# A router rebuilt between two weight streams: logits finished in place, top two by counting, and a gather that comes out transposed

## The chip, the cores and the metric

The kernel runs on one core of a Trainium2 chip. The time is the device time of one execution, in microseconds. It has a TensorE (PE, matrix products; PEld its weight loads), a VectorE (DVE), a ScalarE (ACT), a GpSimd (POOL) and a SyncE (SP), whose queue issues nearly all transfers.

## What is computed

One decoder layer for 256 tokens of width 2048 in fp32. The first part (attention heads beside a gated recurrence) adds its result to x through `w_out`. Then comes a mixture of experts with two-stage routing, and the change lies between the two:

```python
h2 = rms_norm(x, norm_ffn_g)
grp_prob = softmax(h2 @ w_grp + b_grp)            # 4 groups
grp_w, grp_idx = lax.top_k(grp_prob, 1)           # one group
exp_logits = (h2 @ w_er + b_er)[that group]       # 4 experts in it
top_w, top_idx = lax.top_k(softmax(exp_logits), 2)
top_w = top_w / sum(top_w) * grp_w
for each of the 16 experts:
    hid = silu(h2 @ w_gate[e]) * (h2 @ w_up[e]) * combine[:, e]
    out = out + hid @ w_down[e]
x = rms_norm(x + out, final_norm_g)
```

Ties go to the lower index, as in `top_k`.

## The kernel before

**The first part's end.** The projection through `w_out` (`proj_n`, L366) works with split fp32 products: each raw 1 MB tile of weights is cut into a high and a low part (`units`, L319 and L321), and three products are made of them. It goes twice over the columns, once for each half of the contraction. In the second pass the blocks are 512, 512, 512, 256 and 256 columns wide, numbered 0 to 4. Work on a finished block (`out_block`, L688) is a generator in a queue `bgq`: it adds the block to X (L691), squares it for the norm (L694), transposes 128 columns at a time (L705), copies them (L708) and multiplies them with the router's weights (L711), two column groups of the logits at once, into the PSUM tile `pl`. `step(k)` advances the queue by k yields after each unit (L380), `drain()` empties it behind the last projection. All instructions go through a scheduler that keeps program order as priority on each engine, but may bring a ready instruction forward; `keep_in_program_order` forbids this for those so marked.

**The router.** `pl` is copied to SBUF (L735), folded and turned to tokens by two products (L738), scaled by the inverse norm `r2` and biased into `Z` (L746): for each token tile of 128 four groups of four expert logits and one of four group logits, 40 numbers a partition. `first_max` (L752 to L756) takes the first maximum of every four; it runs on `Z`, then, the winner pushed far down (L769), once more. `selb` (L774) holds the two chosen experts of the chosen group. Five small bf16 products count how many earlier tokens chose each expert (L776 to L780): the rank `rk` (L783) is the slot of a token with its expert; each expert has 64 slots (CAP), and a branch at the end, taken if one has more, is not taken with these inputs. `keep_busy` issues filling products on TensorE whose results nobody reads, at three places in this chain.

**The experts.** `gather_matrix(e)` (L846) makes a 0/1 matrix times the inverse norm from ranks. `gather` multiplies it with X, token rows on the output partitions (two column blocks side by side), and copies to SBUF (L860). `turn` transposes that (L834) and multiplies by the norm's gain (L873): `xg`, the expert's inputs with the contraction on the partitions. `stream` multiplies `xg` with four 2 MB pieces of `w_gate`, then of `w_up`. Then come silu (L957), the hidden product (L961), its transposes and copy (L967), and four pieces of `w_down` (`pd`). The result is scattered to tokens behind the next expert's first gate piece (L901). The gather for expert e+1 stands between up and down of expert e. `final_gain` spreads the final norm's gain over the partitions with 16 products, in expert 1 behind the third gate piece.

**The order of transfers.** The list `loads` is an order by hand. Twelve entries are loaded early, most beside the first part, as buffers come free. Piece 8 takes the two raw buffers of the first part as one tile. Later pieces go round a `ring` of nine 2 MB buffers: piece n from 12 on takes the buffer of the piece nine ring places before. Each is issued by `advance()` behind the products that read a piece, and waits in SP's queue for its buffer. Expert 0's last up piece lies outside the ring in a buffer that becomes `rest`, expert 0's hidden values among them.

Of the kernel before, what the change touches and what calls it, by code (L numbers as in the profile page):

```python
# [19 lines left out]
P = 128  # L20
# [17 lines left out]
def hybrid_block_kernel(  # L38
# [149 lines left out]
    rev = cst.tile([P, 4], F32, name="rev")  # L188
    nc.gpsimd.iota(rev, pattern=[[-1, 4]], base=4, channel_multiplier=0,
                   allow_small_or_imprecise_dtypes=True)  # L190
# [51 lines left out]
    def drain():  # L242
        while bgq:
# [6 lines left out]
                   (8, 8), (9, 9), (10, 7), (0, 1, 1)]  # L250
    ring = [d[1] for d in early_loads if len(d) == 2 and d[0] != 7]
# [17 lines left out]
    def load():  # L269
# [96 lines left out]
    def proj_n(aTh, aTl, c0=0, c1=NC, w=512):  # L366
# [3 lines left out]
        while c < c1:  # L370
            for hi, lo in units():
# [8 lines left out]
                step(2 if c0 else 1)  # L380
# [306 lines left out]

    def out_block(b, col, w, pp, last):  # L688
# [10 lines left out]
        for j in range(0, k, 2):  # L699
            xT = xTs[xi[0] % 2]  # L700
            xi[0] += 1
            pt = psmall().rearrange("p (j t) -> p j t", j=2)
            for i in range(2):
                for n in range(NT):
                    nc.tensor.transpose(  # L705
                        pt[:, i, n * P:(n + 1) * P],
                        x2[:, n, bs].rearrange("p (q j) -> p j q", j=k)[:, j + i], ident)
            V.tensor_copy(xT, pt)  # L708
            yield
            for i in range(2):  # L710
                mm(pl[32 * i:32 * i + 32], wr[:, col // P + j + i], xT[:, i],  # L711
                   start=b == 0 and j == 0, stop=b == 4)
# [16 lines left out]
    def keep_busy(k, ps, lhs, rhs):  # L729
        for i in range(k):  # L730
            mm(ps[0:lhs.shape[1], 0:P], lhs, rhs, start=True, stop=True)

    keep_busy(8, busy, ident, x2[:, 1, D - P:])
    lt = dist1[0:64]
    V.tensor_copy(lt, pl)  # L735
    plt = psmall()[:, :40].rearrange("p (n e) -> p n e", n=NT)
    for n in range(NT):
        mm(plt[:, n], lt[:, n * P:(n + 1) * P], fold[0:64], start=True, stop=True)  # L738


    r2 = small8[:, 2:4]
    V.tensor_reduce(r2, ssq, AX.X, ALU.add)
    rstd(r2, r2, D)
    Z = cst.tile([P, 5, NT, 4], F32, name="Z")
    for n in range(NT):
        V.scalar_tensor_tensor(Z[:, :, n], plt[:, n].rearrange("p (g e) -> p g e", g=5),  # L746
# [3 lines left out]
    def first_max(dst, src, m, tmp, vm, k):  # L750

        V.tensor_reduce(m, src, AX.X, ALU.max)  # L752
        V.tensor_tensor(tmp, src, m.unsqueeze(2).to_broadcast([P, k, 4]), ALU.is_equal)
        V.tensor_tensor(tmp, tmp, rev.unsqueeze(1).to_broadcast([P, k, 4]), ALU.mult)
        V.tensor_reduce(vm, tmp, AX.X, ALU.max)
        V.tensor_tensor(dst, tmp, vm.unsqueeze(2).to_broadcast([P, k, 4]), ALU.is_equal)  # L756

    Zf = Z.rearrange("p g n e -> p (g n) e")
    ma = cst.tile([P, 10], F32, name="ma")
    mb = cst.tile([P, 8], F32, name="mb")  # L760
    vm = cst.tile([P, 10], F32, name="vm")
    tmp = cst.tile([P, 10, 4], F32, name="tmp")
    M1 = cst.tile([P, 10, 4], F32, name="M1")
    M2 = cst.tile([P, 8, 4], F32, name="M2")
    E2 = cst.tile([P, 8, 4], F32, name="E2")
    keep_busy(8, busy, Z.rearrange("p g n e -> p (g n e)"), ident)
# [5 lines left out]
    gm = M1[:, 8:10].rearrange("p n g -> p g n").unsqueeze(3).to_broadcast([P, 4, NT, 4])  # L772
# [3 lines left out]
    mm(pr[:, 0], before, selb[:, :, 0], start=True, stop=True)  # L776
    mm(pr[:, 1], ones, selb[:, :, 0], start=True, stop=False)
    mm(pr[:, 1], before, selb[:, :, 1], start=False, stop=True)
    mm(pr[:, 2], ones, selb[:, :, 0], start=True, stop=False)
    mm(pr[:, 2], ones, selb[:, :, 1], start=False, stop=True)  # L780
# [6 lines left out]
    V.tensor_reduce(cmax, pr[:, 2].rearrange("p g e -> p (g e)"), AX.X, ALU.max)  # L787
# [8 lines left out]

    def weights_of_routes():
        V.tensor_tensor(Zf, Zf, ma.unsqueeze(2).to_broadcast([P, 10, 4]), ALU.subtract)
# [6 lines left out]
        V.tensor_tensor(tmp[:, 8:10], Zf[:, 8:10], M1[:, 8:10], ALU.mult)  # L805
# [9 lines left out]
        V.tensor_copy(cmaxi, cmax[:1])  # L815

    cm.release()
# [12 lines left out]
    def mmo(*a, **k):  # L830
        tc.keep_in_program_order(mm(*a, **k))  # L831

    def transpose(dst, src):
        tc.keep_in_program_order(nc.tensor.transpose(dst, src, ident))  # L834

# [6 lines left out]

    def gather_matrix(e):
        pg = mp.tile([P, NT, CAP], F32, name="pg")
        for n in range(NT):
            V.tensor_scalar(pg[:, n], slot[:, :CAP], rk[:, n, e:e + 1], r2[:, n:n + 1],  # L846
                            ALU.is_equal, ALU.mult)
        return pg

    def gather(pg):  # L850

        xn = mp.tile([P, 2, 512], F32, name="xn")
        ps = ptwo("pn")
        for j in range(2):
            for n in range(NT):
                for z in range(2):
                    b = 2 * j + z
                    mmo(ps[64 * z:64 * z + 64, j], pg[:, n], x2[:, n, b * 512:(b + 1) * 512],
                        start=n == 0, stop=n == 1)
            S.activation(xn[:, j], ps[:, j], AF.Copy)  # L860
        return xn

    def turn(xn):
# [12 lines left out]
        return xg  # L876

# [54 lines left out]
    xg = turn(gather(gather_matrix(0)))  # L932
    weights_of_routes()
# [198 lines left out]
```

## Time and profile before

| what | value |
|---|---|
| median of 3 runs | 1419.67 us (1419.36 to 1420.41) |
| profiled execution | 1415.9 us, its span 1414.1 us |
| TensorE busy | 1322.3 us, 94% of the span |
| VectorE, ScalarE busy | 432.9 us, 275.3 us |
| transfers | 483.75 MB, mean 342 GB/s |
| granted TensorE clock, mean | 0.996 |

Times in the rows count from the span's start. The mixture of experts begins near 490 us and lasts to the end; the router lies before it, between about 474 and 485 us. An instruction with fp32 operands stands in the trace as two rows, so counts of products are doubled (a transpose is one row).

### The profile page before, as it was taken

What the parts mean: (1) busy time and instruction counts of PE and PEld (TensorE: products, weight loads), DVE (VectorE), ACT (ScalarE), POOL (GpSimd) and SP (SyncE); (2) the same over time, 40 slices, a digit from 0 to 9 for tenths busy, and PEclk for the clock granted to TensorE, in tenths of its full rate; (3) what the DMA queues carried; (4) which work ended last, traced back from release to release, by engine and by line L of the source; (5) the groups of instructions that cost most, each with busy time, mean ns of one, the idle gap of its engine ahead of it and who ended that gap; (6) DMA issues with size and microseconds to landing.
All of it is one profiled execution on the core that took longest, in us unless ns stands there. A gap on an engine that the chain in (4) does not pass through costs nothing.

```text
span 1414.1 us, 16501 instructions
## 1 busy us (share of the span) xinstructions
PE 1322.3 (94%) x7091; PEld 721.7 (51%) x7091; DVE 432.9 (31%) x647; ACT 275.3 (19%) x409; POOL 17.5 (1%) x47
## 2 busy tenths in 40 slices
PE   9999999999999999999999999889898998989885
PEld 8999998998887633333333323223232232322323
DVE  5555567567555411121121112111121111211012
ACT  5553542542543201000000000000000000000002
POOL 2000000000000000000000000000000000000002
PEclk9999999999999999999999999999999999999998
DMA  6655553455687599999999999999999999999995
GB/s 237 241 163 173 179 173 126 157 183 185 222 338 286 219 409 378 427 428 428 427 428 427 429 427 427 428 429 428 426 430 427 428 427 427 428 427 429 427 410 197
DMA packets 85726, 483.75 MB, mean 342 GB/s; under 512 B 16849, under 2 KB 19601, under 8 KB 60817
## 3 DMA queue, kind: packets, MB, share of 16 engines
q1 hardware_dynamic: 85520, 482.62, 84.6%
q8 instruction: 57, 0.93, 0.3%
q14 instruction: 21, 0.16, 0.0%
q10 hardware_dynamic: 128, 0.03, 0.0%
HBM read 480.54 MB, written 2.10 MB: 341 GB/s over the span
## 4 chain that ended last, share of the span: by engine, by line
PE 66%; DMA 29%; DVE 2%; ACT 2%; issue 1%; ACTq 0%; SPq 0%; DVEq 0%
DMA wt<-in_w_up_dram 25%; PE pd L831 12%; PE pp L340 12%; PE up L831 8%; PE ga L831 6%; PE pp L376 5%; PE pp L377 5%; PE pp L378 5%; PE pn L831 4%; DMA wt<-in_w_gate_dram 3%; PE pt L834 2%; PE pw L482 1%; PE psc L831 1%; DVE rest L967 1%; ACT xn L860 1%
## 5 line engine op out<-in xcount | busy, mean ns | idle before, releaser
L831 PE MATMUL up<-wt,xg 128*64 128x512 f32 x1024 | 231.2, 597 | 38.4 <-DMA wt<-in_w_up_dram 38.4
L831 PE MATMUL ga<-wt,xg 128*64 128x512 f32 x1024 | 226.8, 595 | 4.2 <-DMA wt<-in_w_gate_dram 4.2
L831 PE MATMUL pd<-wt,rest 128*64 128x512 f32 (+1 forms) x1088 | 224.7, 569 | 2.8 <-ACT rest L1016 2.0
L321 DVE TENSOR_TENSOR whl<-sh,whl 128x1024 fp32r<-128x1024 f32 (+1 forms) x145 | 175.5, 1216 | 121.9 <-ACT whl L319 116.8
L319 ACT ACTIVATE whl<-sh 128x1024 fp32r<-128x1024 f32 (+1 forms) x145 | 151.7, 1051 | 223.4 <-PE pp L378 106.0
L340 PE MATMUL pp<-hTh,whl 128*128 128x256 f32 x1024 | 190.4, 285 | 0.0
L831 PEld LDWEIGHTS up<-wt,xg 128*64 128x64 f32 x1024 | 69.4, 137 | 188.1 <-issue 120.3
L340 PEld LDWEIGHTS pp<-hTh,whl 128*128 128x128 f32 x1024 | 161.3, 192 | 0.2
L831 PEld LDWEIGHTS ga<-wt,xg 128*64 128x64 f32 x1024 | 72.9, 137 | 153.7 <-issue 149.8
L831 PEld LDWEIGHTS pd<-wt,rest 128*64 128x64 f32 x1088 | 76.2, 137 | 139.2 <-issue 128.9
L340 PE MATMUL pp<-hTl,whl 128*128 128x256 f32 x512 | 145.2, 284 | 1.1 <-DVE hTl L394 1.0
L901 DVE TENSOR_TENSOR rest<-rest,psc 128x1024 f32<-128x1024 f32 x28 | 34.2, 1221 | 254.4 <-PE psc L831 253.0
L340 PEld LDWEIGHTS pp<-hTl,whl 128*128 128x128 f32 x512 | 98.2, 192 | 1.9 <-DVE hTl L394 1.7
L887 DVE COPY pT<-pt 128x256 f32<-128x256 f32 x16 | 6.8, 424 | 292.5 <-PE pt L834 292.5
L376 PE MATMUL pp<-whl,hTh 128*128 128x512 f32 x192 | 77.5, 404 | 0.0
L860 ACT ACTIVATE xn<-pn 128x512 f32<-128x512 f32 x32 | 19.1, 597 | 295.6 <-PE pn L831 295.6
L378 PE MATMUL pp<-whl,hTl 128*128 128x512 f32 x192 | 75.3, 392 | 0.0
L377 PE MATMUL pp<-whl,hTh 128*128 128x512 f32 x192 | 74.9, 390 | 0.0
L831 PE MATMUL pn<-X,pg 128*64 128x512 f32 x256 | 61.2, 599 | 13.1 <-ACT xn L860 12.4
L831 PE MATMUL psc<-rest,pT 64*128 64x512 f32 x240 | 63.7, 628 | 7.0 <-DVE rest L901 7.0
L957 ACT ACTIVATE rest<-ga 128x512 f32<-128x512 f32 x16 | 9.6, 597 | 281.3 <-PE ga L831 253.6
L981 ACT ACTIVATE rest<-pd 128x1024 f32<-128x1024 f32 x15 | 15.4, 1025 | 234.3 <-PE pd L831 234.3
(273 smaller groups left out, 977.6 us busy)
## 6 DMA issues: line engine op xcount, KB each, us to landing
wt<-in_w_gate_dram SPq DMA_DIRECT2D x63, 2048.0 KB, 39.1
wt<-in_w_up_dram SPq DMA_DIRECT2D x60, 2048.0 KB, 34.9
wt<-in_w_down_dram SPq DMA_DIRECT2D x59, 2048.0 KB, 36.9
sh<-in_w_in_dram SPq DMA_DIRECT2D x55, 1024.0 KB, 5.1
sh<-in_w_out_dram SPq DMA_DIRECT2D x16, 1024.0 KB, 5.7
wt<-in_w_down_dram SPq DMA_DIRECT2D x8, 1024.0 KB, 14.7
wt<-in_w_up_dram SPq DMA_DIRECT2D x8, 1024.0 KB, 28.8
wt<-in_w_gate_dram SPq DMA_DIRECT2D x2, 1024.0 KB, 10.8
```

Source lines behind the costliest of these rows:

```text
L319: S.activation(t[:, 0, a:b], rw, AF.Copy)
L321: V.tensor_tensor(t[:, 1, a:b], rw, t[:, 0, a:b].bitcast(F32), ALU.subtract)
L340: r = mm(*a, **kw)
L376: mm(pp[:, n], ah, hi[:, k], start=c == c0, stop=False)
L377: mm(pp[:, n], ah, lo[:, k], start=False, stop=False)
L378: mm(pp[:, n], al, hi[:, k], start=False, stop=c == c1 - 1)
L482: mm(pa[:, 2 * h + n], k[:, h, ts], q[:, h, ts].rearrange("p (b z m) -> p b z m", z=2, m=m)[:, :, 1], start=True, stop=True)
L831: tc.keep_in_program_order(mm(*a, **k))
L834: tc.keep_in_program_order(nc.tensor.transpose(dst, src, ident))
L860: S.activation(xn[:, j], ps[:, j], AF.Copy)
L901: V.tensor_tensor(acc[n][:, bs], x2[:, n, bs] if e == 0 else acc[n][:, bs], ps.rearrange("p z f -> p (z f)"), ALU.add)
L981: S.activation(osb, pd, AF.Copy)
```

## The change

The last two column blocks, 256 wide, get four steps a unit. Block 3 then also sums the first four squares, copies `pl` and folds it into the token-wise PSUM tile. Block 4 is transposed with tokens apart, two transposes and a copy for each token tile, and its logits are added in place to that tile with the transposed block as the stationary side, 20 columns streaming. The inverse norm is made with one instruction fewer.

The top two come by counting: three instructions over 160 elements compare each logit with the three beside it (a tie counts for the lower index), a reduction gives a rank, and rank 0 is the group, rank below 2 the experts. Maximum and weights are made later (`weights_of_routes`, behind the first piece of `xg`), the largest count too. Filling products are 3, 6 and 3, in program order.

Expert 0 has its gather in transposed form: X's columns are stationary, in quarters with a stride of four, and the gather matrix streams 64 columns; block 0 and half of block 1 come before the first gate piece, the rest behind the first and second. The gather of expert 1 is moved behind expert 0's down projection. `gather` takes two tiles of one bank instead of one of two banks. `final_gain` moves from expert 1 to 6. Piece 8 is loaded as two halves.

```diff
     early_loads = [(1, 0), (2, 1), (3, 4), (4, 5), (5, 2), (6, 3), (0, 0, 0), (7, 6),
-                   (8, 8), (9, 9), (10, 7), (0, 1, 1)]
-    ring = [d[1] for d in early_loads if len(d) == 2 and d[0] != 7]
+                   (8, 0, "raw"), (8, 1, "raw"), (9, 9), (10, 7), (0, 1, 1)]
+    ring = [0, 1, 4, 5, 2, 3, 8, 9, 7]
...
-            wt = single(s, [P, 2048], name="wt")
+            wt = shared[8][:, hf] if s == "raw" else single(s, [P, 2048], name="wt")
...
-                step(2 if c0 else 1)
+                step(4 if w == 256 else 2 if c0 else 1)
...
+            xj = x2[:, :, bs].rearrange("p n (q j) -> p n j q", j=k)
+            if b == 4:
+                for n in range(NT):
+                    pn = psmall()[:, 0:2 * P].rearrange("p (j t) -> p j t", j=2)
+                    for i in range(2):
+                        transpose(pn[:, i], xj[:, n, j + i])
+                    V.tensor_copy(xT[:, :, n * P:(n + 1) * P], pn)
+                for n in range(NT):
+                    for i in range(2):
+                        mmo(plt[0][:, n], xT[:, i, n * P:(n + 1) * P],
+                            wr[:, col // P + j + i, 0:20], start=False, stop=i == 1,
+                            skip_group_check=True)
+                return
...
+        if b == 3:
+            V.tensor_reduce(sq4, ssq[:, :, 0:4], AX.X, ALU.add)
+            V.tensor_scalar(sq4, sq4, EPS * D, None, ALU.add)
+            lt = dist1[0:64]
+            V.tensor_copy(lt, pl)
+            plt[0] = psmall()[:, :40].rearrange("p (n e) -> p n e", n=NT)
+            for n in range(NT):
+                mm(plt[0][:, n], lt[:, n * P:(n + 1) * P], fold[0:64], start=n == 0, stop=False,
+                   skip_group_check=True)
             yield
...
-    keep_busy(8, busy, ident, x2[:, 1, D - P:])
...
+    keep_busy(3, busy, ident, ident)
     r2 = small8[:, 2:4]
-    V.tensor_reduce(r2, ssq, AX.X, ALU.add)
-    rstd(r2, r2, D)
+    V.tensor_tensor(r2, sq4, ssq[:, :, 4], ALU.add)
+    V.reciprocal(r2, r2)
+    S.activation(r2, r2, AF.Sqrt, scale=float(D))
...
-    first_max(M1, Zf, ma, tmp, vm, 10)
-    keep_busy(6, busy, M1.rearrange("p a e -> p (a e)"), ident)
-    V.scalar_tensor_tensor(E2, M1[:, 0:8], -1e30, Zf[:, 0:8], ALU.mult, ALU.add)
-    first_max(M2, E2, mb, tmp[:, 0:8], vm[:, 0:8], 8)
-    V.tensor_tensor(M2, M2, M1[:, 0:8], ALU.add)
+    keep_busy(6, busy, Z.rearrange("p g n e -> p (g n e)"), ident)
+    V.tensor_tensor(wins, zo, zs, ALU.is_gt)
+    V.tensor_tensor(ties, zo, zs, ALU.is_ge)
+    V.copy_predicated(wins, tri.unsqueeze(1).to_broadcast([P, 10, 4, 4]), ties)
+    V.tensor_reduce(rank, wins, AX.X, ALU.add)
+    V.tensor_scalar(G1n, rank[:, 8:10], 0.0, None, ALU.is_equal)
...
-    V.tensor_tensor(selb, M2.rearrange("p (g n) e -> p g n e", g=4), gm, ALU.mult)
+    V.scalar_tensor_tensor(selb.rearrange("p g n e -> p (g n) e"), rank[:, 0:8], 2.0,
+                           G1.unsqueeze(2).to_broadcast([P, 8, 4]), ALU.is_lt, ALU.mult)
...
+    keep_busy(3, busy, ident, ident)
...
-    V.tensor_reduce(cmax, pr[:, 2].rearrange("p g e -> p (g e)"), AX.X, ALU.max)
...
+    def gather_turned(xg, pg, b, q0, q1, pt):
+        xb = x2[:, :, b * 512:(b + 1) * 512].rearrange("t n (p q) -> t n q p", q=4)
+        for q in range(q0, q1):
+            for n in range(NT):
+                mmo(pt[:, q], xb[:, n, q], pg[:, n], start=n == 0, stop=n == 1)
+        if q1 == 4:
+            xg_made.append(V.tensor_tensor(
+                xg[:, 4 * b:4 * b + 4], pt,
+                gfe[:, 4 * b:4 * b + 4].unsqueeze(2).to_broadcast([P, 4, CAP]), ALU.mult).ins)
...
-    xg = turn(gather(gather_matrix(0)))
-    weights_of_routes()
+    pg = gather_matrix(0)
+    cmax_of_ranks()
...
+    gather_turned(xg, pg, 0, 0, 4, pturn())
+    pt1 = pturn()
+    gather_turned(xg, pg, 1, 0, 2, pt1)
...
         for i in stream(ga, xg, e, 0):
+            if e == 0 and i == 0:
+                gather_turned(xg, pg, 1, 2, 4, pt1)
+                gather_turned(xg, pg, 2, 0, 4, pturn())
+                with tc.issue_after(xg_made[0]):
+                    weights_of_routes()
+            if e == 0 and i == 1:
+                gather_turned(xg, pg, 3, 0, 4, pturn())
...
-            if i == 2 and e == 1:
+            if i == 2 and e == 6:
                 gf = final_gain()
...
-        if e + 1 < NE:
+        if 0 < e < NE - 1:
             xn = gather(pg)
...
-        if e + 1 < NE:
+        if 0 < e < NE - 1:
             xg = turn(xn)
...
+        if e == 0:
+            xg = turn(gather(pg))
```

## Rows read from the trace of the kernel before

**Rows 1.** Busy time by window: per engine, clock, transfer share, GB/s.

```profile
580.00:1360.00 780.00, 717.98 (x3268) 241.55 (x3266) 123.44 (x204) 40.31 (x57) 0.00 (x0) 1.00 1.01 427
...
550.00:555.00 5.00, 5.00 (x27) 1.88 (x24) 0.00 (x0) 0.00 (x0) 0.00 (x0) 1.00 0.66 246
560.00:565.00 5.00, 5.00 (x26) 1.72 (x24) 0.00 (x0) 0.60 (x1) 0.00 (x0) 1.00 0.91 315
1000.00:1020.00 20.00, 15.92 (x72) 4.73 (x70) 0.94 (x3) 0.60 (x1) 0.00 (x0) 1.00 1.01 428
```

**Rows 2.** Timeline of SP's queue, issues of pieces 22, 23, 24 and 29.

```profile
551.09 0.33 SPq L285 DMA_DIRECT2D wt<-in_w_down_dram  x1
554.52 0.33 SPq L285 DMA_DIRECT2D wt<-in_w_down_dram  x1
561.92 0.33 SPq L285 DMA_DIRECT2D wt<-in_w_gate_dram  x1
...
586.45 0.33 SPq L285 DMA_DIRECT2D wt<-in_w_up_dram  x1
```

**Rows 3.** Timeline from the last projection product to the logits Z.

```profile
474.32 0.28 PE L378 MATMUL pp<-whl,oT 128*128 128x256 f32 x1
...
474.64 0.75 DVE L691 TENSOR_TENSOR X<-X,pp 128x256 f32<-128x256 f32 x2 [5.81 <-PE pp L378]
...
475.12 0.76 PEld L705 LDWEIGHTS pw<-ident,X 128*128 128x128 f32 x4 [0.22 <-DVE X L691]
...
480.02 0.38 DVE L746 SCALAR_TENSOR_TENSOR Z<-pw,small,bias 128x20 f32<-128x20 f32 x2 [1.50 <-PE pw L738]
```

**Rows 4.** Chain that ended last, router: start, length, what.

```profile
470.98 0.56 PE pl L711 x4
...
474.61 0.48 PE pw L705 x4
...
479.36 0.56 PE pw L738 x4
```

**Rows 5.** VectorE's groups by form: busy, mean ns of one.

```profile
L753 DVE TENSOR_TENSOR tmp<-Z,ma 128x40 f32<-128x40 f32 x1 | 0.2, 199 | 0.0
...
L501 DVE TENSOR_TENSOR sh<-sh 128x128 f32<-128x128 f32 x2 | 0.6, 292 | 0.1
...
L505 DVE COPY_PREDICATED sh<-mask,pw 128x512 f32<-128x512 uint8 x10 | 9.4, 945 | 0.0
```

**Rows 6.** Timeline, end of the router and expert 0's gather.

```profile
483.16 0.19 DVE L774 TENSOR_TENSOR selb<-M,M 128x32 bf16<-128x32 f32 x1
...
484.62 1.94 PE L831 MATMUL pn<-X,pg 128*64 128x512 f32 x8 [0.70 <-PE pw L780]
```

**Rows 7.** Chain that ended last, experts 0 and 1.

```profile
490.68 13.88 PE ga L831 x64
...
518.81 1.74 PE pn L831 x8
521.29 1.94 PE pn L831 x8
524.78 0.73 PE pt L834 x4
525.51 13.88 PE pd L831 x64
...
554.48 3.82 PE pt L831 x32
```

**Rows 8.** Timeline of TensorE in the recurrence: stationary 128x128, 64 columns.

```profile
220.76 1.89 PE L482 MATMUL pw<-sg,sh 128*128 128x64 f32 x16
```

**Rows 9.** Timeline, hidden products of experts 0 and 15, last down.

```profile
519.49 0.69 DVE L961 TENSOR_TENSOR rest<-rest,up 128x512 f32<-128x512 f32 x1 [6.72 <-ACT rest L957]
...
1375.68 0.69 DVE L961 TENSOR_TENSOR rest<-rest,up 128x512 f32<-128x512 f32 x1 [9.27 <-PE up L831]
...
1377.95 2.38 PE L831 MATMUL pd<-wt,rest 128*64 128x256 f32 x20 [0.78 <-DVE rest L967]
```

More of the change, by code (lines that the diff above doesn't have):

```diff
@@ L187, in hybrid_block_kernel @@
                                 base=-32 * j, pattern=[[-1, 20]], channel_multiplier=1)
-    rev = cst.tile([P, 4], F32, name="rev")
-    nc.gpsimd.iota(rev, pattern=[[-1, 4]], base=4, channel_multiplier=0,
-                   allow_small_or_imprecise_dtypes=True)
+    trif = cst.tile([P, 4, 4], F32, name="trif")
+    nc.gpsimd.memset(trif, 1.0)
+    nc.gpsimd.affine_select(out=trif, in_=trif, compare_op=ALU.is_ge, fill=0.0, base=-1,
+                            pattern=[[1, 4], [-1, 4]], channel_multiplier=0)
+    tri = cst.tile([P, 4, 4], U8, name="tri")
+    nc.gpsimd.tensor_copy(tri, trif)
     ssq = cst.tile([P, NT, 5], F32, name="ssq")
@@ L686, in hybrid_block_kernel, with mmo, transpose @@
     x2 = X
+    def mmo(*a, **k):
+        tc.keep_in_program_order(mm(*a, **k))
+    def transpose(dst, src):
+        tc.keep_in_program_order(nc.tensor.transpose(dst, src, ident))
+    plt = [None]
+    sq4 = small8[:, 4:6]
     def out_block(b, col, w, pp, last):
@@ L711, in out_block @@
                 mm(pl[32 * i:32 * i + 32], wr[:, col // P + j + i], xT[:, i],
-                   start=b == 0 and j == 0, stop=b == 4)
+                   start=b == 0 and j == 0, stop=b == 3)
+            yield
+        if b == 3:
[7 more added lines that the diff above has]
+                   skip_group_check=True)
             yield
@@ L730, in keep_busy @@
         for i in range(k):
-            mm(ps[0:lhs.shape[1], 0:P], lhs, rhs, start=True, stop=True)
-    keep_busy(8, busy, ident, x2[:, 1, D - P:])
[L734 to L738, printed above, removed]
+            mmo(ps[0:lhs.shape[1], 0:P], lhs, rhs, start=True, stop=True)
+    keep_busy(3, busy, ident, ident)
     r2 = small8[:, 2:4]
-    V.tensor_reduce(r2, ssq, AX.X, ALU.add)
@@ L773, in hybrid_block_kernel @@
+    gm = G1.rearrange("p (g n) -> p g n", n=NT).unsqueeze(3).to_broadcast([P, 4, NT, 4])
     selb = cst.tile([P, 4, NT, 4], BF16, name="selb")
-    V.tensor_tensor(selb, M2.rearrange("p (g n) e -> p g n e", g=4), gm, ALU.mult)
+    V.scalar_tensor_tensor(selb.rearrange("p g n e -> p (g n) e"), rank[:, 0:8], 2.0,
+                           G1.unsqueeze(2).to_broadcast([P, 8, 4]), ALU.is_lt, ALU.mult)
     pr = psmall()[:, :48].rearrange("p (a g e) -> p a g e", a=3, g=4)
-    mm(pr[:, 0], before, selb[:, :, 0], start=True, stop=True)
@@ L777, in hybrid_block_kernel @@
[L777 to L780, printed above, removed]
+    mmo(pr[:, 0], before, selb[:, :, 0], start=True, stop=True)
+    mmo(pr[:, 1], ones, selb[:, :, 0], start=True, stop=False)
+    mmo(pr[:, 1], before, selb[:, :, 1], start=False, stop=True)
+    mmo(pr[:, 2], ones, selb[:, :, 0], start=True, stop=False)
@@ L781, in hybrid_block_kernel @@
+    mmo(pr[:, 2], ones, selb[:, :, 1], start=False, stop=True)
+    keep_busy(3, busy, ident, ident)
     rk = cst.tile([P, NT, 4, 4], F32, name="rk")
@@ L930, in final_gain, with pturn @@
         return gf
-    xg = turn(gather(gather_matrix(0)))
-    weights_of_routes()
+    pg = gather_matrix(0)
+    cmax_of_ranks()
+    xg = mp.tile([P, NC, CAP], F32, name="xg")
+    def pturn():
+        return pscr()[:, 0:256].rearrange("p (q s) -> p q s", q=4)
+    gather_turned(xg, pg, 0, 0, 4, pturn())
+    pt1 = pturn()
+    gather_turned(xg, pg, 1, 0, 2, pt1)
     pend = None
```

49 lines of the change are left out of this document (24 added, 25 removed).

## The prediction, made before the changed kernel had run

> **What bounds the kernel now.** I read the stretches by window first. From 580 to 1360 us, one row for the whole stretch, the transfer engines move 427 GB/s with a share of 1.01, and in a stretch within it TensorE is busy 15.9 of 20 us [rows 1]. The reader is to see that the rate of the part is that of the whole. So this part is bound by the weight stream, and a faster TensorE there is worth nothing. What can be won is time in which the stream stands still because no buffer is free: in the rows of 550 to 555 and 560 to 565 it runs at 246 and 315 GB/s [rows 1].
>
> The queue of SP came next, because each weight transfer is issued there when TensorE has released its buffer. I number the 2048 KB pieces in order of use, twelve to an expert, from 0. A piece read from the ring is replaced by the one nine places on in the ring, so piece 22 waits for piece 13 (second gate piece of expert 1), 23 for 14, 24 for 15, 29 for 20. Their issues are the four rows [rows 2]. One piece takes 2.097 MB / 427 GB/s = 4.91 us. Each issue sets a floor for the end: its time plus 4.91 us for each piece after it. Piece 24, issued at 561.92, sets the highest floor. Piece 29 at 586.45 is level with it (561.92 + 5 x 4.91 = 586.47). Piece 22 at 551.09 lies 561.92 - 9.82 - 551.09 = 1.01 us below, piece 23 at 554.52 2.5 us below. From piece 30 on the floors fall away, since TensorE needs less for an expert than the stream. So the end moves only if the issues of 22, 23, 24 and 29 all move, and by the worst of them.
>
> **The change part by part.** I work out when TensorE releases piece 13.
>
> *The last logits.* Before, the transposes and logits of column block 3 are done after the last projection product, which starts at 474.32 [rows 3]. With four steps a unit instead of two they are issued among the products of block 4. TensorE streams there without a gap, so they push the last product: transposes 0.48, logits 0.56, and the fold, which now is among them, 0.56 [rows 4], together 1.6 us; with the overlap of a first load I take 1.5. Bounds: 0, if all of it falls into the wait for the adds behind the last product, and 1.6. After the last product: the two adds start at 474.64 and the transposes at 475.12, as before [rows 3], done by 476.0; a copy for each token tile, 128x256 at 0.42 (the adds, of that size, took 0.75 for two, overlapping [rows 3]), the second from 476.05 to 476.47; four weight-stationary instructions for the second tile at the 0.14 of the fold [rows 4], to 477.1; Z at 477.2 in place of 480.02 [rows 3]. The inverse norm, three small instructions of about 0.2 us, ends then too. Gone from the path are the second copy, the fold and the filling products ahead of it. Sum: -2.8 + 1.5 = -1.3 us.
>
> *Top two by counting.* From Z at 480.02 [rows 3] to the end of selb at 483.16 + 0.19 [rows 6] it was 3.33 us. Now six instructions follow Z, three of them and a reduction over 160 elements. 40 elements take 199 ns and 128 take 292 ns [rows 5], a slope of 1.06 ns, so 160 take 0.33. The trace has the predicated copy at 945 ns for 512 elements [rows 5]: between 0.30 in proportion and 0.40 with a fixed part; I take 0.40. Z 0.40 + 3 x 0.33 + 0.40 + two of 0.19 + five gaps of 0.03 = 2.3 us, -1.0. Taking the maximum of ranks off VectorE's path is counted as nothing. The 3 + 6 + 3 filling products have the durations of the waits (two instructions each, at 0.14 as the fold's [rows 4]: six of them 0.84 and twelve 1.7 us, against 1.27 us from selb to the gather [rows 6] and 1.9 us from Z to selb) and cost nothing; a filler that came late would add at most its 0.84. So expert 0's gather, first instruction 484.62 before [rows 6], starts 2.3 us earlier.
>
> *The transposed gather.* Before, from 484.62 to the first gate product at 490.68 it is 6.06 us [rows 6, 7]. Now there are 32 products, 64 instructions, of a 128x128 fp32 stationary and 64 columns. The nearest row has just this shape: sixteen in 1.89 us, of which the last instruction's 0.28 is tail, 0.108 each [rows 8]. That one reads contiguous rows; here the stationary has a stride of four elements, as the transposes of the block before had, 0.12 each [rows 4]. I take 0.115: 7.4 us, 1.3 more than before, though the gate stream now starts after 24 of the 64. Lower bound 64 x 0.108 = 6.9; upper bound 64 x 0.18 = 11.7, from the four strided transposes of expert 1 that stand alone, 0.73 us [rows 7]. The Trainium skill, "TensorE: Matmul & The Clock Gate", section "LDWEIGHTS (loading the stationary operand)", speaks against this form: a load costs by the columns of the stationary, about 107 ns for 128, whatever streams behind it, so twice the columns are loaded for an eighth of the streaming. By its figure the sum would be 6.8 us, an estimate 0.6 under mine, and the row with 0.108 agrees.
>
> *Expert 1's gather moved behind expert 0's down projection.* Before, up ended at 518.81 and down began at 525.51, 6.70 us, filled with gather and transposes [rows 7]. Expert 0's hidden product ends at 519.49 + 0.69 = 520.18; for the last expert, which has no gather, it takes from 1375.68 + 0.69 to 1377.95, 1.58 us, from there to down [rows 9]. So down begins at 521.76, 3.75 earlier. In return expert 1's gate waits behind down for the gather: two halves of 1.94 and two groups of transposes of 0.75, 5.4 us [rows 7]; the copies hide behind the other half. Net +1.65. Pieces 18 to 20, which wait for this down, are asked for 3.75 + 2.3 - 1.3 = 4.7 us sooner, but they did not set the end.
>
> *Separate banks for the two halves of a gather* save a wait (518.81 + 1.74 to 521.29, 0.74 us [rows 7]) for every later expert, under the weight stream: nothing. *Final gain from expert 1 to 6* takes 32 instructions (3.82 us [rows 7]) from before piece 15; at expert 6 it lies where TensorE waits for weights [rows 1]. *Piece 8 in halves* lets 1 MB start earlier, ahead of the experts, where no piece waits for one of TensorE's releases that set the floor: nothing, and if it held up the pieces behind it, at most its own 2.5 us.
>
> **Sum.** Piece 13 is released 2.3 earlier, 1.3 + 1.65 later: 0.65 us later, piece 22 at 551.74. Piece 23 the same, 555.2. Piece 24: 0.65 - 3.8 = 3.2 earlier; 29 too. Now 22 sets the floor, in place of 24, at 1.01 - 0.65 = 0.4 us lower. The profiled execution took 1415.9 us and would take 1415.5. The median of the runs stands 3.8 us above it, at 1419.67, so 1419.3.
>
> **The rivals.**
> *Faster.* The inserted block-3 work slips into holes, or behind the last product (-1.5), the gather runs at 0.108 (-0.5) and the counting chain at its lower bounds (-0.3). Then piece 22 comes 1.6 us earlier than before, the floor falls 2.7 us: 1417.0, and with half a microsecond more past the bound of 0.2%. For it: before, the transposes of block 3 ran free in the wait behind the last product [rows 4]. Against: priority of the earlier work. Chance 0.28.
> *Slower: strided weight loads do not overlap.* At the 0.18 of the lone transposes the gather takes 11.7 us, 4.3 more; piece 22 at 556.0, 3.9 us over the old floor: 1423.6. It decides from 0.165 an instruction, where the loss passes 2.8 us. Against it: the strided transposes at 0.12. Chance 0.15.
> *Slower: the clock.* Fewer fillers and two bare waits around expert 0's hidden product. If the granted clock fell to 1.2 GHz there, down's 13.88 us [rows 7] would double: 14 us, 1433. The trace shows 1.00 in a stretch with four idle microseconds in twenty [rows 1]. Chance 0.04.
> *TensorE sets the end after all*, and 14 gathers shortened by 0.7 us count: 1410. Against: the flat 427 GB/s. Chance 0.03.
> *Nothing much, by the sum above:* 0.50, with its own range from 1417.5 to 1421.5.
>
> **How the numbers follow.** A difference under 0.2%, 2.8 us, is about what a measurement of this kernel can tell from no change. Of the 0.50 all but 0.02, for waits that I placed wrongly, is within it; of the faster case, whose centre lies at the bound, half is beyond, 0.14, with TensorE's 0.03: 0.17. Of the slower cases 0.17 is beyond, with the 0.02: 0.19. Within: 0.64. The range leaves out the clock case and the TensorE case, and the far ends: 1415.6 to 1423.8.
>
> **What would show it.** Z some 3.0 us behind the last product's start and six VectorE instructions to selb in 1.9 us; 64 gather instructions in 7.4 us; expert 1's first gate product within 0.7 us of where it was; and in the queue of SP piece 22 at about 551.7 as the last issue that finds the stream empty, with 427 GB/s from there. It is wrong if pieces 13 and 14 are released more than 3 us off, if the stream halts later than 565 us, or if the clock in the first two experts is under 1.00.

## The result, and the profile after

The changed kernel takes 1431.73 us (median of 6 runs, 1430.65 to 1433.61) against 1419.57 us (6 runs, 1415.53 to 1420.41) for the kernel before on the same chip: a ratio of 1.0094 with an interval of 1.0084 to 1.0105, slower by about 12 us. The profiled execution took 1432.58 us, 16.7 us more than the profiled one of before, its mean granted clock 0.987 in place of 0.996. That 16.7 is more than 12 is in part the choice of execution: on the chips of the experiments, executions of the kernel before with a mean granted clock of 0.996, as the profiled one, took 1414.9 to 1417.8 us, those with 0.993 took 1418.3 to 1419.9, and the profiled execution of the changed kernel has the lowest clock of its six. The range of the prediction ended at 1423.8.

The stretches by window of the changed kernel show first whether the weight stream still sets the end (columns as in [rows 1]):

```profile
580.00:1360.00 780.00, 723.62 (x3284) 246.77 (x3282) 121.66 (x204) 41.22 (x59) 0.00 (x0) 1.00 1.01 428
550.00:555.00 5.00, 5.00 (x26) 1.61 (x24) 0.00 (x0) 1.62 (x2) 0.00 (x0) 1.00 1.03 439
...
560.00:565.00 5.00, 4.53 (x20) 1.40 (x18) 2.80 (x3) 0.00 (x0) 0.00 (x0) 1.00 0.62 213
565.00:570.00 5.00, 5.00 (x26) 1.58 (x24) 1.90 (x2) 0.00 (x0) 0.00 (x0) 1.00 0.48 206
```

The rate from 580 us on is 428 GB/s, 427 before, so the weight stream still sets the pace there. What moved is the place of the hole, where the stream runs short of free buffers: at 565 to 570 us it now runs at half its rate, where before it was back at 429:

```profile
565.00:570.00 5.00, 5.00 (x26) 1.59 (x24) 0.84 (x3) 0.00 (x0) 0.00 (x0) 1.00 1.00 429
```

The queue of SP names the late issue, piece 22:

```profile
569.26 0.33 SPq L289 DMA_DIRECT2D wt<-in_w_down_dram  x1
```

It stood at 551.09 before [rows 2]: 18.17 us later. Less the 1.01 us by which its floor lay under that of piece 24, that is 17.2 us, against the 16.7 measured. So all of the loss lies ahead of this issue. The timeline from the last projection product to the gather:

```profile
477.48 0.28 PE L382 MATMUL pp<-whl,oT 128*128 128x256 f32 x1
...
480.47 0.38 DVE L778 SCALAR_TENSOR_TENSOR Z<-pw,small,bias 128x20 f32<-128x20 f32 x2 [0.57 <-PE pw L694]
...
482.49 0.19 DVE L803 SCALAR_TENSOR_TENSOR selb<-rank,G 128x32 bf16<-128x32 f32 x1
...
483.86 5.68 PEld L694 LDWEIGHTS pt<-pg,X 128*128 128x128 f32 x24 [0.27 <-ACT tmp L854]
```

The gather's first product comes at 483.89, 0.73 us earlier than before [rows 6]. This execution started 1.14 us late (the first weights had landed at 13.82 us, at 12.68 in the profile of before), so the router gained 1.9 us. The chain that ended last tells the rest (start, length, what):

```profile
4.46 9.36 DMA sh<-in_w_in_dram
...
483.89 5.83 PE pt L694 x24
489.73 5.63 PE ga L694 x16
495.35 5.79 PE pt L694 x24
501.15 5.04 PE ga L694 x16
506.19 3.88 PE pt L694 x16
510.06 7.02 PE ga L694 x32
...
531.41 1.28 ACT L1019
534.08 0.76 PE pt L697 x4
535.61 16.91 PE pd L694 x64
552.52 3.43 PE pt L694 x16
556.65 0.75 PE pt L697 x4
557.41 3.58 PE ga L694 x16
```

The gather (`pt` from 483.89, 64 instructions) takes 5.83 + 5.79 + 3.88 = 15.5 us in place of 6.06. Two pieces of the gate take 5.63 and 5.04 us where an undisturbed one (557.41) takes 3.58, and down takes 16.91 where it took 13.88 [rows 7]. The granted clock of these stretches, by window, says why (it is the third value from the end):

```profile
487.00:490.00 3.00, 3.00 (x14) 2.83 (x15) 1.73 (x14) 0.24 (x1) 0.00 (x0) 0.50 0.11 44
490.00:493.00 3.00, 3.00 (x8) 0.70 (x6) 1.11 (x6) 0.00 (x0) 0.00 (x0) 0.50 0.00 0
...
495.00:500.00 5.00, 5.00 (x22) 4.72 (x21) 0.42 (x1) 0.00 (x0) 0.00 (x0) 1.00 0.94 385
...
501.00:504.00 3.00, 3.00 (x9) 0.99 (x10) 0.42 (x1) 0.00 (x0) 0.00 (x0) 0.50 0.00 0
...
535.00:541.00 6.00, 5.39 (x14) 1.70 (x16) 0.56 (x1) 0.00 (x0) 0.00 (x0) 0.50 0.82 350
```

The granted clock falls to 1.2 GHz three times (rows one and two, row four, row five), and in the first two rows TensorE is busy all the time. In the third row the gather runs at 2.4 GHz and its 24 instructions still take 5.79 us: its length is not the clock's.

**The sum.** From the gather's first instruction to the issue of piece 22 it was 551.09 - 484.62 = 66.47 us and is 569.26 - 483.89 = 85.37, 18.9 more. The gather's instructions make 15.50 - 6.06 = +9.44; the gate at the lower clock 17.69 - 13.88 = +3.81; up to down 4.25 in place of 6.70, -2.45; down +3.03; the gather behind down +4.89; the rest +0.2. This stretch is free of the drift of an execution's start, so the experiments are compared by it. In all of them the profiled time less the issue of piece 22 is 862.6 to 864.6 us, so to within 2 us the end follows this issue.

### The profile page after: what moved, and what is told of

The parts are those of the page before. It is cut to its first block, busy times and chain, and to the rows that moved or that the text cites. A ratio compares the mean times of both kernels' runs of the same rounds, so it can differ in the third digit from the quotient of the medians.

```text
span 1430.9 us, 16552 instructions
## 1 busy us (share of the span) xinstructions
PE 1342.8 (94%) x7115; PEld 736.9 (52%) x7115; DVE 434.3 (30%) x644; ACT 274.3 (19%) x408; POOL 17.1 (1%) x49
## 4 chain that ended last, share of the span: by engine, by line
PE 64%; DMA 32%; DVE 2%; ACT 1%; issue 1%; SPq 0%; ACTq 0%; DVEq 0%
DMA wt<-in_w_up_dram 18%; PE pp L344 12%; PE pd L694 10%; DMA wt<-in_w_gate_dram 8%; PE ga L694 8%; PE up L694 7%; DMA wt<-in_w_down_dram 5%; PE pp L380 5%; PE pp L381 5%; PE pp L382 5%; PE pt L694 4%; PE pt L697 2%; PE psc L694 2%; PE pw L486 1%; DMA sh<-in_w_in_dram 1%; DVE rest L947 1%
## 5 line engine op out<-in xcount | busy, mean ns | idle before, releaser
L694 PE MATMUL ga<-wt,xg 128*64 128x512 f32 x1024 | 232.9, 607 | 12.5 <-DMA wt<-in_w_gate_dram 12.5
L895 ACT ACTIVATE xn<-pt 128x512 f32<-128x512 f32 x30 | 17.9, 597 | 274.1 <-PE pt L694 274.1
L1019 ACT ACTIVATE rest<-ga 128x512 f32<-128x512 f32 x16 | 9.6, 597 | 264.7 <-PE ga L694 264.7
L694 PE MATMUL pt<-X,pg 128*64 128x512 f32 x240 | 54.0, 592 | 0.0
```

The lines of the kernel that those rows point to most:

```text
L895: S.activation(xn[:, j], ps, AF.Copy)
```

## The experiments

"A" is the changed kernel, "B" the one before; ratios are to B on the same chip, with their intervals. The last column is the stretch from the gather's first instruction to piece 22 (B 66.47, A 85.37).

| run | from | edit | median us | ratio | gather to piece 22 |
|---|---|---|---|---|---|
| a1_contig | A | gather reads contiguous columns | 1420.72 | 1.0025 (1.0015 to 1.0034) | 74.35 |
| s2_stride2 | A | stride 2 | 1421.8, one run | | 74.59 |
| x3_stride3 | A | stride 3 | 1428.51, one run | | 79.54 |
| x2_stride8 | A | stride 8 | 1432.81, one run | | 85.64 |
| x1_turns | A | transposes in place of products, stride 4 | 1423.65, one run | | 76.14 |
| d1_wide | A | gather streams 128 columns | 1427.63 | 1.0084 (1.0060 to 1.0108) | 80.67 |
| b2_fill | A | fillers around the hidden product | 1430.82 | 1.0101 (1.0081 to 1.0121) | 82.67 |
| c1_both_clock | A | both of these | 1426.82 | 1.0057 (1.0040 to 1.0074) | 78.97 |
| t1_warm_silu | A | Silu's table loaded early | 1429.39 | 1.0080 (1.0063 to 1.0097) | 82.47 |
| a3_move_back | A | expert 1's gather back | 1425.34 | 1.0059 (1.0043 to 1.0076) | 78.52 |
| a2_old_gather0 | A | expert 0's gather as in B | 1415.90 | 0.9989 (0.9979 to 0.9998) | 68.54 |
| a4_both_old | A | both of these | 1411.09 | 0.9957 (0.9940 to 0.9973) | 64.45 |
| b1_gain_only | B | final gain in expert 6 | 1416.23 | 0.9984 (0.9974 to 0.9993) | 66.46 |
| b3_gain_banks | B | that and two tiles of one bank | 1412.92 | 0.9965 (0.9955 to 0.9974) | 64.45 |
| e1_contig_rows | A | contiguous, weights to match, expert 1's gather back | 1416.38 | 0.9988 (0.9977 to 1.0000) | 68.63 |

**What a load costs.** My theory was that the strided loads make the gather's length; the rival, that the clock does.

```diff
-        xb = x2[:, :, b * 512:(b + 1) * 512].rearrange("t n (p q) -> t n q p", q=4)
+        xb = x2[:, :, b * 512:(b + 1) * 512].rearrange("t n (q p) -> t n q p", q=4)
```

(a1_contig; "..." in this and the later cuts marks lines left out; the columns go to other rows of the product, so expert 0's output is another, as in the four runs that follow.)

> The changed kernel, with expert 0's gather reading X's columns in contiguous blocks of 128 instead of with a stride of four; this permutes expert 0's inputs against the rows of its weights, so the output of expert 0 is another. Load theory: the strided fp32 loads (0.24 us an instruction in the trace of after) are the cost; contiguous they take 0.108 to 0.115, the 64 gather instructions 7 us instead of 15.5, and the median comes from 1431.7 to 1423, or to 1419.5 if the clock also holds in the gate pieces. Rival, clock first: the fallen clock makes the loads slow, not the stride; then the instructions stay near 0.24 and the time within 1 us of 1431.7. Rival, moved gather: most of the loss lies behind up of expert 0, so at most 3 us come back.

> The changed kernel with expert 0's gather reading X's columns with a stride of two instead of four elements (which permutes expert 0's inputs against its weights' rows). It measures the load alone: 0.233 us an instruction at stride four, 0.108 to 0.116 contiguous. If the cost grows with the stride, 0.15 to 0.17 and 1425; if any stride costs the same, 0.233 and 1431; if two is free, 0.11 and 1421.

```diff
-        xb = x2[:, :, b * 512:(b + 1) * 512].rearrange("t n (p q) -> t n q p", q=4)
+        xb = x2[:, :, b * 512:(b + 1) * 512].rearrange("t n (h p q) -> t n h q p", h=2, q=2)
...
-                mmo(pt[:, q], xb[:, n, q], pg[:, n], start=n == 0, stop=n == 1)
+                mmo(pt[:, q], xb[:, n, q // 2, q % 2], pg[:, n], start=n == 0, stop=n == 1)
```

The later three ask what in the stride costs, because groups of four transposes at stride four stand at about 0.13 an instruction in the kernel before.

> The changed kernel with each product of expert 0's transposed gather replaced by two transposes of the same 128 columns at stride four (its output for expert 0 is another). The stationary reads are the same, the operation is not. Theory that the stride alone costs: 24 loads in 5.6 us, 0.233 each. Rival: a transpose's load is not slowed, as the short groups of transposes at stride four stand at about 0.13 in the kernel before: 24 in 2.8 to 3.4 us, and then it is the product in fp32 with a strided stationary that pays.

```diff
-                mmo(pt[:, q], xb[:, n, q], pg[:, n], start=n == 0, stop=n == 1)
+                for k in range(2):
+                    transpose(pt[:, q], xb[:, n, q])
...
```

> The changed kernel with the columns of expert 0's gather at a stride of eight elements, 32 bytes, in place of four (its output for expert 0 is another). If what costs is that every element lies in another 16 bytes, stride eight costs the same as stride four: 24 loads in 5.7 us. If the cost grows with the distance: 9 to 11 us.

```diff
-        xb = x2[:, :, b * 512:(b + 1) * 512].rearrange("t n (p q) -> t n q p", q=4)
+        c0 = b // 2 * 1024
+        xb = x2[:, :, c0:c0 + 1024].rearrange("t n (p q) -> t n q p", q=8)[
+            :, :, b % 2 * 4:b % 2 * 4 + 4]
```

> The changed kernel with the columns of expert 0's gather at a stride of three elements, 12 bytes (its output for expert 0 is another). If the load pays for each 16 bytes that it touches, 96 for 128 elements, it takes 0.75 of 0.233, 0.175 us: 24 loads in 4.2 us. If every stride over two pays in full: 5.6 us. If only a stride of 16 bytes pays: 2.9 us.

```diff
-        xb = x2[:, :, b * 512:(b + 1) * 512].rearrange("t n (p q) -> t n q p", q=4)
+        xb = [x2[:, :, b * 512 + q:b * 512 + q + 382:3] for q in range(4)]
...
-                mmo(pt[:, q], xb[:, n, q], pg[:, n], start=n == 0, stop=n == 1)
+                mmo(pt[:, q], xb[q][:, n], pg[:, n], start=n == 0, stop=n == 1)
```

One group of 24 loads from the timeline of each, in the order contiguous, stride 2, stride 3, stride 8, and last the transposes at stride 4:

```profile
490.00 2.75 PEld L694 LDWEIGHTS pt<-pg,X 128*128 128x128 f32 x24 [0.81 <-issue]
```

```profile
490.98 2.90 PEld L694 LDWEIGHTS pt<-pg,X 128*128 128x128 f32 x24 [0.81 <-issue]
```

```profile
495.72 4.29 PEld L694 LDWEIGHTS pt<-pg,X 128*128 128x128 f32 x24 [0.81 <-issue]
```

```profile
495.22 5.79 PEld L694 LDWEIGHTS pt<-pg,X 128*128 128x128 f32 x24 [0.81 <-issue]
```

```profile
491.05 2.96 PEld L697 LDWEIGHTS pt<-ident,X 128*128 128x128 f32 x24 [0.81 <-issue]
```

Divided by 24 these are 0.115, 0.121, 0.179, 0.241 us, and 0.123 for the transposes; the changed kernel has 0.237 (5.68 / 24). Stride eight costs what stride four does, so the distance does not matter. Stride three touches 96 pieces of 16 bytes with 128 elements, three quarters as many as stride four, and costs three quarters (0.179 of 0.237). These five fit a product's load that pays for each 16 bytes touched, above a bottom near 0.11. So strided loads make the gather's length, as the theory had it; the 5.7 us expected at stride eight and the 4.2 at stride three came true, and at stride two the load is all but free. In x1_turns the rival came true, the transposes do not pay: the operation matters beside the stride, and not the length of the group, since they too were 24 in a row. Why a transpose is spared stays open.

The Trainium skill, "SBUF — State Buffer", section "Door 1: The DMA port swizzle (why `[64,N]` ≈ `[32,N]`)", has a note that fits the products: SBUF is read in lines of 16 bytes, two accesses or more to a line run at full rate, and each step to a new line pays. The strides of one, two, four and eight agree with it; the transposes, at stride four, do not. The same note lets one "stride for free" up to "4 fp32"; for the loads of products that does not hold (0.179 at stride three, 0.237 at four).

Contiguous loads alone take the stretch 11.0 us down, from 85.37 to 74.35: 8 us of loads, and the clock kept at 1.00 through the gate's pieces. Both rivals of this run fall with that, no change and at most 3 us. The faster loads do not bring the gate forward by the whole of it. The timeline of a1_contig:

```profile
485.77 1.94 PE L694 MATMUL ga<-wt,xg 128*64 128x512 f32 x8
...
488.13 1.94 PE L694 MATMUL ga<-wt,xg 128*64 128x512 f32 x8 [0.42 <-DMA wt<-in_w_gate_dram]
```

The second half of the gate's first piece has only just landed then. A faster gather would have met this wait next.

**The clock.** Two runs take away, one each, what I held to be the reasons for the falls.

```diff
-                mmo(pt[:, q], xb[:, n, q], pg[:, n], start=n == 0, stop=n == 1)
+                mmo(pt[:, q], xb[:, n, q], pg[:, n].unsqueeze(1).to_broadcast([P, 2, CAP]),
+                    start=n == 0, stop=n == 1)
...
```

> The changed kernel with expert 0's gather streaming 128 columns instead of 64 for each strided load (the gather matrix twice over, the second copy unread): the same loads, twice the columns. Load theory: an instruction stays at 0.233 us, since the load sets its pace. If the streamed columns decide the granted clock, it stays at 1.00 in more of the gate pieces and up to 3.8 us come back, 1428; if the loads set the clock, or the gap to full streaming is still too large, the dips stay and the time is within 1 us of 1431.7.

```diff
+        if e == 0:
+            pf = ptwo("pf")
+            for k in range(3):
+                mmo(pf[:, 0], ident, x2[:, 0, 0:512], start=True, stop=True)
         pt = pscr().rearrange("p (j s) -> p j s", j=4)
...
         V.tensor_copy(hT, pt)
+        if e == 0:
+            mmo(pf[:, 1], ident, x2[:, 0, 0:512], start=True, stop=True)
```

> The changed kernel with four filling products (128x128 by 512 columns, nobody reads them) in the two bare waits between expert 0's up and down projections: three ahead of the transposes, one ahead of down. Theory: the clock fell there because TensorE stood idle for 2.75 us and did little before and after; with the waits filled it holds at 1.00, down takes 13.9 instead of 16.9 us, and the median falls by 3 us, to 1428.7. Rival: the fall comes from the gather's phase or is nothing that idling decides; then down stays near 16.9 us and the time within 1 us of 1431.7.

> The changed kernel with the wide gather stream and the four fillers of the two runs before it together. If the two stretches at the lower clock are separate losses, both savings add: piece 22 at 569.26 - 5.9 - 3.8 = 559.6 us and a profiled time of 863.2 + 559.6 = 1422.8 us, with the granted clock at 1.00 from 486 to 546 us. What is then left above the old kernel is the strided loads (some 8 us) less the router's gain. Rival: the two share one cause, so that the second remedy adds little: piece 22 near 563, 1426 us.

With twice the columns behind each load (d1_wide) the loads stay as long (5.67 us for 24), and the clock stays up. Windows of d1_wide:

```profile
486.00:489.00 3.00, 3.00 (x15) 2.59 (x17) 1.88 (x14) 0.24 (x1) 0.00 (x0) 1.00 0.05 19
489.00:492.00 3.00, 3.00 (x16) 0.82 (x12) 0.97 (x5) 0.00 (x0) 0.00 (x0) 1.00 0.25 46
```

The stretch gets 4.7 us shorter. With the wait before down filled (b2_fill), down is back at 13.88 us at clock 1.00, and the stretch is 2.7 us shorter; the falls in the gather remain. The chain of b2_fill:

```profile
534.85 13.88 PE pd L694 x64
```

Together they save 6.4, not 7.4, since in d1_wide down's excess is already smaller (15.65 in place of 16.91). c1_both_clock came out at piece 22 at 562.82 and 1426.1 profiled, nearer to the rival's numbers than to mine; but I had taken the savings from issue times that held 1.1 us of drift each, and by the stretch the two add but for 1.0 us. In c1_both_clock the clock is 1.00 from 486 to 546 us, and the stretch is still 78.97, 12.5 over B.

**Silu's table.** In the chain of the changed kernel a ScalarE table load of 1.28 us (L1019) stands behind up, and TensorE waits for it. Before, the same load ran far ahead of the wait, straight behind the gather's last copy; ScalarE's timeline of before:

```profile
489.89 1.28 ACT L957 ACT_TABLE_LOAD   x1
```

```diff
         S.activation(Zf, Zf, AF.Exp)
+        S.activation(vm[:, 0:1], Zf[:, 0, 0:1], AF.Silu)
```

> The changed kernel with one more ScalarE instruction, a Silu on one column behind the exponential of the routing weights, whose result nobody reads. Theory: Silu's table load, 1.28 us at 531.41 in the changed kernel, stands behind the wait for up only because no ScalarE work lies between the exponential and Silu; with the early Silu it comes near 490 us under the gather. Then up to down of expert 0 is 4.27 - 1.28 = 2.99 us, as it is in the run with the old first gather (2.93), and piece 22 comes 1.3 us earlier from there, up to 3 us more if the shorter wait spares the clock the fall in down. From the gather's first instruction to piece 22: 84.1, or 82 to 83 with the clock, in place of 85.4. Rival: the table load moves, but down's dip stays at 16.9 us: 84.1 exactly. Second rival: the load is wanted again at expert 0's Silu: 85.4.

ScalarE's timeline of this run:

```profile
489.67 1.28 ACT L837 ACT_TABLE_LOAD   x1
...
531.79 0.60 ACT L1020 ACTIVATE rest<-ga 128x512 f32<-128x512 f32 x1 [40.63 <-PE up L694]
```

The load now lies under the gate. Up to down takes 2.93 us, down 15.65 in place of 16.91, the stretch 82.47: the theory, with a part of the clock's fall given back. The first rival falls with down's time, the second with the row at 531.79. Why the load behind the exponential does not run ahead of the wait, as it did behind the copy, is not shown.

**Expert 1's gather, and the versions that are faster.**

```diff
-        if 0 < e < NE - 1:
+        if e < NE - 1:
             xn = gather(pg)
...
-        if 0 < e < NE - 1:
+        if e < NE - 1:
             xg = turn(xn)
...
-        if e == 0:
-            xg = turn(gather(pg))
```

> The changed kernel with expert 1's gather back between expert 0's up and down projections; the transposed gather of expert 0 stays. Load theory: 4.9 us behind down go, 2.4 come back ahead of it, and the clock holds in down (3.0): 5.5 us less, 1426.2. Rival, moved gather: 10 us less or more, 1421.7 or below.

```diff
...
-    gather_turned(xg, pg, 0, 0, 4, pturn())
-    pt1 = pturn()
-    gather_turned(xg, pg, 1, 0, 2, pt1)
+    xg = turn(gather(pg))
+    weights_of_routes()
...
```

> The changed kernel with expert 0's gather as before (rows, copy, transposes); everything else as changed. Load theory: 15.5 us of gather become 6.1 and the clock holds in the first gate pieces (3.8 us): 13.2 us less, 1418.5. Rival, moved gather: at most 4 us less, 1427.7 or above.

> The changed kernel with both gathers as before: what is left of the change is the routing chain, the fillers, the separate banks, the final gain in expert 6 and piece 8 in halves. Load theory with the floors of the transfer queue: piece 13 is released 0.7 us earlier than in the profiled execution of before, piece 24 asked for 4.5 us earlier, so the floor falls by 1.0 + 0.7 = 1.7 us: a profiled execution of 1414.2, and a median at or under that of before, 1414 to 1418. Rival: the routing chain or the early transfers carry part of the loss: 1421 or more.

By the stretch a3_move_back gives 6.9 us back, where the load theory had 5.5 and its rival 10 or more; a2_old_gather0 gives 16.8 back, where the theory had 13.2 and the rival at most 4. The 3.6 us more are the old gather in 5.07 us, not 6.1 (the banks, below), and 1.3 us each of the wait before down and of down. a4_both_old came out at 1411.07 profiled, 3.1 under the 1414.2 expected; 2.0 of these are the banks'.

The chain of a2_old_gather0 and then of a4_both_old, from up to expert 1's gate:

```profile
510.07 7.04 PE up L694 x32
518.51 0.77 PE pt L697 x4
...
520.04 15.65 PE pd L694 x64
535.69 3.43 PE pt L694 x16
...
540.57 3.58 PE ga L694 x16
```

```profile
509.77 7.02 PE up L694 x32
516.78 3.43 PE pt L694 x16
...
522.43 13.88 PE pd L694 x64
536.31 3.43 PE ga L694 x16
```

The move alone costs 68.54 - 64.45 = 4.1 us here: down comes 2.7 us sooner, the gather takes 4.9 behind it, and down runs 1.8 longer, since its clock falls behind a bare wait of 2.93 us. With the gather in that wait down is 13.88. The version with both old gathers, and all else of the change, beats both kernels: 1411.09 us. The new router and piece 8 in halves were not tried alone; the router's 1.9 us are read from the trace.

**The banks and the gain, alone.**

```diff
-        ps = ptwo("pn")
         for j in range(2):
+            ps = pscr()
...
-            if i == 2 and e == 1:
+            if i == 2 and e == 6:
```

> The kernel before with the final gain moved from expert 1 to expert 6 and nothing else. By the prediction's floors piece 24 is asked for 3.8 us earlier, piece 22 is not, and its floor lies 1.0 us lower: 1.0 us less than the kernel before, near 1416.6. Then the separate banks make the other 3.5 to 4 us of the run that had both. Rival: the banks are worth nothing, as the prediction had it, and the gain makes all of it: near 1413.

> The kernel before with two parts of the change alone: the final gain in expert 6, and one bank for each half of a gather. The floors: the gain releases piece 15 3.8 us earlier, so piece 22 sets the end and 1.0 us are won; the banks save about 1 us in expert 0's gather and 1 us in expert 1's, both ahead of piece 13, so 2 more: 3.0 us under the kernel before. Rival, as the prediction had it: the banks count for nothing, 1.0 us in all.

b1_gain_only is the second pair of lines alone. The gain does what the floors say: the stretch to piece 22 is unchanged, 66.46, and the median is 2.3 us under B's, with 1.0 to 3.7 allowed by the interval, where 1.0 was worked out. The chain of b3_gain_banks:

```profile
485.88 3.65 PE pt L831 x16
...
490.97 13.88 PE ga L831 x64
...
519.10 3.43 PE pt L831 x16
...
524.75 13.88 PE pd L831 x64
```

The banks take 2.0 us from the stretch, a microsecond at each of the two gathers ahead of piece 22: from the gather's start to the gate 490.97 - 485.88 = 5.09 in place of 6.06, and from up to down 5.65 in place of 6.70. The expectation of b1_gain_only left them 3.5 to 4, that of b3_gain_banks 2, which is what the stretch shows. But the median of b3_gain_banks lies 4.9 us under B's (3.7 to 6.4 by the interval), not 3.0; the other 1.9 have no cause shown.

**A transposed gather without the stride.**

```diff
+        if kind < 2 and e == 0:
+            return (w_gate, w_up)[kind][0, e].rearrange("(b q p) f -> p b q f", p=P, q=4)[
+                :, i, a:b, :]
...
-        xb = x2[:, :, b * 512:(b + 1) * 512].rearrange("t n (p q) -> t n q p", q=4)
+        xb = x2[:, :, b * 512:(b + 1) * 512].rearrange("t n (q p) -> t n q p", q=4)
...
-                gfe[:, 4 * b:4 * b + 4].unsqueeze(2).to_broadcast([P, 4, CAP]), ALU.mult).ins)
+                gffn[:, 4 * b:4 * b + 4].unsqueeze(2).to_broadcast([P, 4, CAP]), ALU.mult).ins)
...
```

> The changed kernel with expert 0's transposed gather from contiguous columns, the rows of expert 0's gate and up pieces loaded in the order that goes with it (2 KB runs in place of 8 KB), and expert 1's gather back between up and down of expert 0. With loads at 0.11 and no bare wait, piece 22 should come at 557.3 - 7.1 = 550.3 us: 1413.3 profiled, some 2 us over the version with both old gathers, since 64 loads take 7.0 us where the old gather took 5.1. Rival: the shorter runs slow the eight transfers of expert 0, and its gate waits for weights: later than 552, 1415 or more.

The chain of this run:

```profile
477.80 11.53 DMA wt<-in_w_gate_dram
489.38 1.94 PE ga L697 x8
491.31 2.82 PE pt L697 x24
```

Piece 22 came at 552.15, later than the 550.3 expected: the rival's side. The stretch is 4.2 us over that of a4_both_old. The gate's second half waits for weights until 489.38, where the old gather in separate banks (a4_both_old) has the gate begun at 488.65 and running without a stop; and 64 loads take 7.6 us even from contiguous columns. The transfer takes 11.53 us from the chain's row, 10.83 in a1_contig with its longer runs. Whether the shorter runs make that difference, one execution each doesn't settle.

## Why the prediction was wrong

**The model held.** The floors of the transfer queue, piece 22 as the one that sets the end, and the sum against the profiled time are right to within 2 us in every run; what was wrong went into the sum as prices. By the prediction the stretch from the gather to piece 22 was to be 66.47 + 1.3 + 1.65 = 69.4 us; it is 85.4. Of the 16 us between, the transposed gather makes 8.1, the clock 6.8 and a table load 1.3, less 0.5 at the gather behind down.

**The router** was right: 1.9 us sooner at the gather where 2.3 were worked out, Z 480.47 - 477.48 = 2.99 us behind the last product's start (predicted some 3.0), 2.21 us from Z to the end of `selb` (2.3). Only the push of the last product was mis-sized: 477.48 - 474.32 - 1.14 = 2.0 us, not 1.5, and above my upper bound of 1.6.

**The transposed gather is the step that failed.** "... here the stationary has a stride of four elements, as the transposes of the block before had, 0.12 each" is wrong twice. Block 3 is 256 wide, so its transposes have a stride of two (k = w // P); and a transpose is not a product: at stride four it takes 0.123, a product 0.237. The price of 0.115 should have been twice that, and with it 15.5 us in place of 7.4. My rival of strided loads was right in kind, and its chance of 0.15 was too small; its bound of 0.18 came from lone groups of transposes, so that even this bound lay below the measured value, and the range with it. The Trainium skill, "TensorE: Matmul & The Clock Gate", section "LDWEIGHTS (loading the stationary operand)", has a load cost by its columns alone; that nearly holds at a stride of one or two (0.115 and 0.121 us), and not at three or more.

**The clock** was given 0.04 and a whole down at half speed. It fell at three places, for some microseconds each, and cost 6.8 us in all, of which down has 3.0, not 14. That this rival's 1433 lies next to the measured 1431.73 is chance. I had looked at stretches with idle time, and the two falls in the gather came where TensorE was busy without a gap, but with loads and few columns.

**Expert 1's gather** was to cost 1.65 us net. In the changed kernel up to down, gather behind down and down itself give -2.45 + 4.89 + 3.03 = 5.5. The gather behind down is 0.5 better than its price, which the banks explain. Up to down is 1.3 worse: the end of the hidden product, 520.18, was taken from the trace of before, where Silu's table was long loaded, and in the changed kernel the load stands behind up; t1_warm_silu gives it back. The 1.58 us from there to down held (534.04 to 535.61). The rest is the clock.

**The banks** were put at nothing "under the weight stream". The gathers of experts 0 and 1 lie ahead of piece 22, and the change gave a microsecond at each in the kernels that keep both. In the changed kernel only one of them is left, so that this did not change the sum by more than the half microsecond above.

**The final gain** was right: piece 24 no longer sets the end, and 22 does.

**From the profile to the median** the prediction added the 3.8 us by which the median of before stood above its profiled execution. In the changed kernel the median stands 0.85 us below the profiled one. So the profiled time was missed by 17.1 us (1415.5 predicted), the median by only 12.4: this term hid 4.6 us of the miss, by luck.

## What to carry to other kernels

Take the price of an instruction from a row of the same operation with the same stride; transposes and products of one shape differ by a factor of two at stride four. Where work is turned from streaming columns into loading stationaries, look at the granted clock behind it, and where work is taken out of a wait, at what the wait was covering on every engine: here a table load and the clock. A change of several parts is best timed part by part: those kept in a4_both_old gained 6 us, and the two new gathers lost more than three times as much.

## What the hardware did that I had not expected

A load of 128 fp32 columns for a product took 0.115, 0.121, 0.179, 0.237 and 0.241 us at strides of 1, 2, 3, 4 and 8 elements; for a transpose 0.123 at stride 4. The granted clock fell to 0.50 while PE and PEld were both shown busy throughout, and stayed at 1.00 when the same loads had 128 columns behind them in place of 64.

The clock also fell in the router itself in three of the fourteen profiled executions with the new chain (t1_warm_silu, x2_stride8, x3_stride3). A window of x2_stride8 there:

```profile
481.00:482.00 1.00, 1.00 (x6) 0.91 (x5) 0.44 (x3) 0.00 (x0) 0.00 (x0) 0.50 0.88 377
```

The filling products then outlast the wait, and the gather starts 5.9 us behind the last logits' first product, not 4.6. Up to this place these kernels have the same instructions as the others, and the clock is 1.00 there in the other eleven; what makes the difference was not tried.
